# Issuing one layer's raw weight loads from the scalar engine's DMA queue instead of SyncE's

## The chip, the cores and the metric

The kernel runs on one core of a Trainium2 chip. Its time is the device time of one execution in microseconds (us); of several executions the median is given. A core has a matrix engine (PE, with PEld for its weight loads), a vector engine (DVE), a scalar engine (ACT), GpSimd (POOL) and SyncE (SP). SP computes nothing here: it issues DMA transfers. Each engine has one queue of instructions, which it works through in order. An instruction whose semaphore is not there yet holds up all that stands behind it on its engine.

## The reference, cut to what matters

Two layers over a sequence of 512 tokens of width 2048, all in float32. Each layer normalises its input, mixes, multiplies by large weight matrices and adds a gated result. Layer 0 is an attention with forget gates, layer 1 a recurrence (RWKV-7).

```python
for i in range(DEPTH):                                   # DEPTH = 2
    mod = c_act @ w_mod[i] + b_mod[i]
    shift, scale, gate = jnp.split(mod, 3, axis=-1)
    h = rms_norm(x, norm_w[i]) * (1.0 + scale[:, None, :]) + shift[:, None, :]
    ...                                                  # layer 0: fox_branch, layer 1: rwkv7_branch
    x = x + gate[:, None, :] * out

def rwkv7_branch(h, v_first, mu, w_in, ...):             # layer 1
    xx = jnp.pad(h[:, :-1], ((0, 0), (1, 0), (0, 0))) - h
    xr, xk, xv, xg = (h + xx * mu[i] for i in (0, 2, 3, 5))          # and xw, xa
    r = xr @ w_in[0]; k = xk @ w_in[1]; v = xv @ w_in[2]; z = xg @ w_in[3]
    ...                                                  # decay, v, a: small matrices (lora)
    _, y = lax.scan(step, S0, xs)                        # the recurrence over 512 tokens, 32 heads
    ...                                                  # group norm, bonus
    return (y * jax.nn.silu(z)) @ w_out
```

Layer 1 has five 2048 x 2048 matrices: `r`, `k`, `v`, `z` (the gate) and the output.

## The kernel before

**Three matmuls for one.** A float32 product is made of three faster ones. Both operands are split: a high half, which ACT makes by a copy into a shorter format (`act_hi`), and a low half, the rest, which DVE makes by a subtraction. `mm3` then multiplies high by high, low by high and high by low.

**Tiles, units, parts.** Layer 1's matrices are worked through in 74 output tiles of 128 columns: the last 10 tiles of `k` (the first 6 are made by an earlier stage), then 16 each of `r`, `v`, `z` and the output. A tile has 16 units (a unit is 128 rows of the matrix, one `mm3`), and 4 units are one part: 128 x 512 numbers, 256 KB. There are 296 parts. `backbone` goes over the units in a fixed order. At the change from one matrix to the next two tiles are interleaved.

**What a part needs.** `fetch(n)` brings part n. It takes one of three raw buffers (`raw`, `bufs=3`), has SP load the part from memory, and after 4.5 us of the planner's own clock it traces the split: ACT writes `whi`, DVE then writes `wlo` from `raw` and `whi`. Buffers of `whi` and `wlo` are four each. A raw buffer is free again when `wlo` has been written, so the load of part n waits for `wlo` of part n-3. `fetch(n)` is started at the first unit of part n-4. The first four parts are fetched ahead of the first unit, one whole `fetch` after the other: load, `whi`, `wlo`, load, `whi`, `wlo`, and so on.

**The other work.** Between the units the planner (`Flow`) traces the rest of layer 1 as tasks with due times, counted on PE's work: copies of finished tiles, the lora products, the keys with their norms (`keys`: square `sq`, halves `mhi` and `mlo`, a matmul for the mean, then `t`), 32 x 32 inverses, and the recurrence (`stage`, `products`, `recur`, `normed`). Nearly all of it goes through ACT at some point. Results wait in memory between the stages, and SP issues all of those transfers too.

**What sets the order.** `InOrder` wraps an engine. While its `on` is set, each instruction of the engine is put behind the one traced before it. It is set for PE, ACT and DVE in layer 1, and not for SP: the scheduler of the framework orders SP's transfers by its own estimate of when each can start, so a load whose buffer is free may be issued long before the place where it was traced. The wrapper takes every call on the engine, `dma_start` as well:

```python
def __getattr__(self, name):
    f = getattr(self.engine, name)
    def issue(*a, **k):
        with ExitStack() as s:
            if self.on and self.last is not None:
                s.enter_context(self.tc.issue_after(self.last.ins))
            self.last = f(*a, **k)
```

All transfers that SP and ACT issue count on the same eight completion semaphores, in turn, in the order of the schedule. The program makes a transfer wait until the one that used its semaphore before, eight transfers earlier, has landed.

Of the kernel before, what the change touches and what calls it, by code (L numbers as in the profile page):

```python
# [21 lines left out]
WK = 4  # L22
# [109 lines left out]
def body(ctx, tc, a, out, dbg=None, stop=0):  # L132
    nc = tc.nc
    pe, act, dve, pool, sp = (InOrder(tc, e) for e in (nc.tensor, nc.scalar, nc.vector,
                                                       nc.gpsimd, nc.sync))
# [23 lines left out]
    def bank(tag, bufs=None):  # L159
        return cur["p"].tile([P, T], F, tag=tag, bufs=cur["t"][tag], name=tag)  # L160
# [71 lines left out]
    def act_hi(hi, src):  # L232
        act.activation(hi, src, AF.Copy)
# [19 lines left out]
    def mm3(o, w, k, x, first, last, m0=0, m1=P):  # L253
        wh, wl = w
        xh, xl = x
        pe.matmul(o, wh[:, k, m0:m1], xh, start=first, stop=False)
        pe.matmul(o, wl[:, k, m0:m1], xh, start=False, stop=False)
        pe.matmul(o, wh[:, k, m0:m1], xl, start=False, stop=last)
# [30 lines left out]
    def silu_c(mp):  # L289
        cb = mp.tile([P, D], F, name="cb", bufs=1)  # L290
        cs = mp.tile([P, KT], F, name="cs", bufs=1)
        i = act.activation(cs, vecs[:, V_C], AF.Silu)
        return cb, cs, i
# [22 lines left out]
    freed, spent = set(), set()  # L316
    PLEAD = 4

    def backbone(fl, tiles, at, ready, ends, pairs=(), lead=6, pre=()):

        units, i = [], 0
        while i < len(tiles):
            us = [[(n, k) for k in range(t[4] if len(t) > 4 else 0, KT)]
                  for n, t in enumerate(tiles[i:i + 1 + (i in pairs)], i)]
            units += us[0][:PLEAD] if len(us) > 1 else us[0]
            for u, v in zip(us[0][PLEAD:], us[1] if len(us) > 1 else ()):
                units += [u, v]  # L330
            if len(us) > 1:
                units += us[1][KT - PLEAD:]
            i += len(us)
        starts = {}
        for i, k in units:
            starts.setdefault((i, k // WK), (i, k))
        parts = list(starts)
        ws, used = {}, set()

        def fetch(n):  # L340
            i, h = parts[n]
            raw = wp.tile([P, WK, P], F, tag="raw", name="raw", bufs=3)
            sp.dma_start(raw, tiles[i][0][:, h * WK:h * WK + WK, :])
            yield 4.5
            while n and parts[n - 1] not in ws or n > 3 and parts[n - 4] not in used:
                yield 0.2
            hi = wp.tile([P, WK, P], R, tag="whi", name="whi")
            lo = wp.tile([P, WK, P], R, tag="wlo", name="wlo")
            act_hi(hi, raw)
            yield 1  # L350
            dve.tensor_tensor(out=lo, in0=raw, in1=hi, op=OP.subtract)
            ws[parts[n]] = hi, lo

        def ending(task, i):
            yield from task
            freed.add(i)

        for n, w in enumerate(pre):
            ws[parts[n]] = w
        for n in range(len(pre), 4):  # L360
            for _ in fetch(n):
                pass
        for n in range(4, len(parts)):
            at.setdefault(starts[parts[n - 4]], []).append(fetch(n))
        last = {id(t[1]): i for i, t in enumerate(tiles)}
        banks, seen = {}, set()
        for i, k in units:
            src, acts, done, j = tiles[i][:4]
            first = i not in seen
            while first and i > 1 and i - 2 not in freed:  # L370
                fl.t += 0.2
                fl.run()
            if first:
                seen.add(i)
                banks[i] = bank("pj")
                at.setdefault((i, max(k, KT - lead)), []).append(ending(done(j, banks[i], i), i))
            for t in at.pop((i, k), ()):
                fl.start(fl.t, t)
            fl.run()
            while (id(acts), k) not in ready or (i, k // WK) not in ws:  # L380
                fl.t += 0.2
                fl.run()
            mm3(banks[i], ws[i, k // WK], k % WK, acts[k], first, k == KT - 1)
            if k % WK == WK - 1:
                used.add((i, k // WK))
            if last[id(acts)] == i:
                spent.add((id(acts), k))
            if k == KT - 1:
                ends.add(i)
# [6 lines left out]
    with ExitStack() as s0:  # L396
# [7 lines left out]
        with tc.tile_pool(name="st0", bufs=2, reuse_waits="tile") as q:  # L404
# [97 lines left out]
            cb, cs, i = silu_c(cbp)  # L502
# [91 lines left out]
            pre = [zw[3 * NZ + j] for j in range(4)]  # L594
# [3 lines left out]
        fl = Flow()  # L598
        freed.clear()
        ends, cut, lock, sdone, odone, gdone, ready = (set() for _ in range(7))  # L600
# [314 lines left out]
        tiles = [(a["wz"][j], A, zfin, j, KT - WK) for j in range(NZ)]  # L915
# [7 lines left out]
        at = {}  # L923
        n = len(tiles)
        at[n - 2, 0] = [gathering()]
        ready |= {(id(A), k) for k in range(KT)}
        tiles += [(a["wo0"][j], G, output, j) for j in range(KT)]
        backbone(fl, tiles, at, ready, ends, {n - 2, n}, pre=pre)
        fl.drain()
        gst.close()  # L930
# [121 lines left out]
    fl = Flow()  # L1052
# [13 lines left out]
    ends, ups, vd, qd, rd, yd, zd = (set() for _ in range(7))  # L1066
# [756 lines left out]
    ready = {(id(A), k) for k in range(KT)}  # L1823
    at = {}
    tiles = [(a["wk1"][j], A, kept, j) for j in range(KT - NK, KT)]
# [8 lines left out]
    n0, n1, n2, n3 = NK, NK + KT, NK + 2 * KT, NK + 3 * KT  # L1834
    for n, task in ((n0, mixing(1, Ar, A)), (n1, mixing(0, Av, Ar)), (n2, mixing(2, Az, Av)),
                    (n3, gathering())):
        at[n - 2, 0] = [task]
    backbone(fl, tiles, at, ready, ends, {n - i for n in (n0, n1, n2, n3) for i in (0, 2)}, 14)
    fl.drain()


def build(nc, arrays, dbg=(), stop=0):
    a = {k: nc.dram_tensor("in_" + k, v.shape, mybir.dt.from_np(v.dtype),
                           kind="ExternalInput").ap() for k, v in arrays.items()}
    out = nc.dram_tensor("out_0_dram", (KT, P, T), F, kind="ExternalOutput").ap()
    d = {k: nc.dram_tensor("dbg_" + k, s, F, kind="ExternalOutput").ap() for k, s in dbg}
    with tile.TileContext(nc) as tc, ExitStack() as ctx:
        body(ctx, tc, a, out, d, stop)
    return out
# [11 lines left out]
```

## Time and profile before

| | |
|---|---|
| median of 3 runs | 2402.3 us (2398.12 to 2408.5) |
| the profiled execution's own time | 2401.73 us |
| its span in the profile | 2399.9 us |
| mean granted PE clock | 0.982 |
| DMA, mean over the span | 200 GB/s, 480.23 MB |
| layer 1's `backbone` on PE | about 1179 to 2396 us |

The profile is one execution. "Busy" is the time in which an engine works on an instruction; issuing a DMA is not busy time. A row of a timeline has the start in us from the span's beginning, the duration, the engine, the operation, what it writes and reads, a count where rows are merged, and in brackets the idle time just before it with what ended it. A row of the waits has the engine and what it was about to write, what it waited for, and the total in us, the number of times and the longest. In the rows of a window "(x)" is the number of instructions, PEclk the share of the full clock that PE was granted, and the DMA share the mean busy share of the core's 16 DMA engines. `SPq` is a DMA that SP issues. All instructions carry the line of a helper (L90), so groups are told apart by the names of tiles.

### The profile page before, as it was taken

What the parts mean: (1) busy time and instruction counts of PE and PEld (TensorE: products, weight loads), DVE (VectorE), ACT (ScalarE), POOL (GpSimd) and SP (SyncE); (2) the same over time, 40 slices, a digit from 0 to 9 for tenths busy, and PEclk for the clock granted to TensorE, in tenths of its full rate; (3) what the DMA queues carried; (4) which work ended last, traced back from release to release, by engine and by line L of the source; (5) the groups of instructions that cost most, each with busy time, mean ns of one, the idle gap of its engine ahead of it and who ended that gap; (6) DMA issues with size and microseconds to landing.
All of it is one profiled execution on the core that took longest, in us unless ns stands there. A gap on an engine that the chain in (4) does not pass through costs nothing. (4 is left out here: it accounts for less than half of the span.)

```text
span 2399.9 us, 39413 instructions
## 1 busy us (share of the span) xinstructions
PE 2302.2 (96%) x13626; PEld 1807.3 (75%) x13626; DVE 1605.2 (67%) x2850; ACT 1256.5 (52%) x2300; POOL 694.4 (29%) x1114
## 2 busy tenths in 40 slices
PE   6999999999999999998999898899999899999999
PEld 4787777877778778886777676677777677777787
DVE  6886778888888635336797567666476776755322
ACT  4435655555565545225646777763345556665221
POOL 0002333442424210110141208771245535450000
PEclk8999999999999999999999999899999999999999
DMA  8864466766666346445756999886867766544543
GB/s 307 328 227 156 128 211 217 222 213 213 205 224 220 114 161 225 142 141 157 223 179 198 308 263 277 256 252 187 233 187 195 219 174 194 167 132 154 161 137 97
DMA packets 388152, 480.23 MB, mean 200 GB/s; under 512 B 146032, under 2 KB 217840, under 8 KB 384112
## 3 DMA queue, kind: packets, MB, share of 16 engines
q1 hardware_dynamic: 386288, 475.08, 63.7%
q0 software_dynamic: 1664, 2.63, 0.3%
q8 instruction: 108, 1.77, 0.3%
q14 instruction: 92, 0.75, 0.1%
HBM read 381.63 MB, written 95.95 MB: 199 GB/s over the span
## 5 line engine op out<-in xcount | busy, mean ns | idle before, releaser
L90 PE MATMUL pj<-hi,whi 128*128 128x512 f32 x2416 | 987.4, 409 | 11.0 <-ACT hi L90 8.2
L90 PE MATMUL pj<-hi,wlo 128*128 128x512 f32 x2416 | 959.4, 397 | 10.1 <-DVE wlo L90 10.0
L90 PE MATMUL pj<-lo,whi 128*128 128x512 f32 x2416 | 959.9, 397 | 0.0
L90 DVE TENSOR_TENSOR wlo<-raw,whi 128x512 fp32r<-128x512 f32 (+2 forms) x628 | 473.4, 761 | 255.1 <-ACT whi L90 252.4
L90 ACT ACTIVATE whi<-raw 128x512 fp32r<-128x512 f32 (+2 forms) x628 | 393.9, 634 | 399.0 <-PE pj L90 215.1
L90 PEld LDWEIGHTS pj<-hi,whi 128*128 128x128 f32 x2416 | 459.5, 190 | 116.8 <-ACT hi L90 9.2
L90 PEld LDWEIGHTS pj<-lo,whi 128*128 128x128 f32 x2416 | 458.3, 190 | 108.4 <-DVE lo L90 0.7
L90 PEld LDWEIGHTS pj<-hi,wlo 128*128 128x128 f32 x2416 | 459.9, 190 | 105.2 <-DVE wlo L90 13.4
L90 DVE CUSTOM_DVE_ANT_0 wm<-wm,cb 128x1024 f32<-128x1024 f32 x128 | 155.8, 1217 | 0.3
L90 POOL TENSOR_SCALAR SV<-SV,dec 64x64 f32<-64x64 f32 x224 | 94.2, 442 | 103.9 <-DVE SV L90 69.7
L90 ACT ACTIVATE pr<-Sm,mx 128x128 f32<-128x128 f32 (+3 forms) x128 | 71.5, 559 | 76.8 <-POOL mx L90 76.3
L90 POOL TENSOR_SCALAR pr<-pr,rc 128x128 f32<-128x128 f32 (+3 forms) x128 | 100.8, 788 | 26.0 <-DVE rc L90 23.6
L90 POOL TENSOR_SCALAR mx<-mx 128x1 f32<-128x1 f32 x128 | 59.9, 468 | 143.2 <-DVE mx L90 98.0
L90 DVE CUSTOM_DVE_ANT_0 Sm<-S,cmask 128x128 f32<-128x128 f32 (+3 forms) x128 | 62.3, 487 | 42.5 <-PE S L90 41.8
L90 POOL TENSOR_TENSOR lt<-lane 128x30 f32<-128x30 f32 (+14 forms) x90 | 64.2, 713 | 86.4 <-DMA lane<-mld 79.6
L90 POOL TENSOR_TENSOR bk<-bk,eI 128x512 f32<-128x512 f32 x32 | 36.6, 1142 | 110.3 <-PE S L90 64.0
L90 POOL TENSOR_TENSOR lane<-lane,lt 128x30 f32<-128x30 f32 (+14 forms) x90 | 64.0, 711 | 7.0
L90 PE MATMUL S<-k,q 128*128 128x128 f32 (+7 forms) x256 | 61.9, 323 | 0.0
L90 POOL TENSOR_TENSOR acc<-acc,sq 128x512 f32<-128x512 f32 x14 | 18.1, 1296 | 149.4 <-ACT sq L90 128.2
L90 ACT ACTIVATE pT<-tr 128x512 f32<-128x512 f32 x64 | 31.0, 485 | 54.4 <-PE tr L90 54.4
L90 DVE SCALAR_TENSOR_TENSOR hp<-pj,gate,hp 128x512 f32<-128x512 f32 x16 | 12.0, 751 | 68.0 <-PE pj L90 68.0
L90 PE MATMUL tr<-ident,pr 128*128 128x128 f32 x320 | 56.0, 273 | 1.5 <-DVE pT L90 1.3
(325 smaller groups left out, 3284.0 us busy)
## 6 DMA issues: line engine op xcount, KB each, us to landing
wm<-in_wmodT SPq DMA_DIRECT2D x132, 512.0 KB, 4.4
raw<-in_wz SPq DMA_DIRECT2D x128, 256.0 KB, 3.7
raw<-in_wo SPq DMA_DIRECT2D x128, 256.0 KB, 3.6
raw<-in_wv SPq DMA_DIRECT2D x124, 256.0 KB, 3.9
wm<-in_wmodT SPq DMA_DIRECT2D x30, 1024.0 KB, 6.4
raw<-in_wk SPq DMA_DIRECT2D x96, 256.0 KB, 3.7
raw<-in_wr SPq DMA_DIRECT2D x64, 256.0 KB, 5.0
raw<-in_wq SPq DMA_DIRECT2D x56, 256.0 KB, 3.5
```

The lines of the kernel that those rows point to most:

```text
L90: self.last = f(*a, **k)
```

## The change

`backbone` gets a parameter for the engine that issues the raw loads. Layer 0 keeps SP. Layer 1's call passes `act`, so its 296 raw loads become instructions of ACT's queue, and as `act.on` is set they keep the place in ACT's order in which `fetch` traces them.

```diff
-    def backbone(fl, tiles, at, ready, ends, pairs=(), lead=6, pre=()):
+    def backbone(fl, tiles, at, ready, ends, pairs=(), lead=6, pre=(), ld=sp):
...
         def fetch(n):
             i, h = parts[n]
             raw = wp.tile([P, WK, P], F, tag="raw", name="raw", bufs=3)
-            sp.dma_start(raw, tiles[i][0][:, h * WK:h * WK + WK, :])
+            ld.dma_start(raw, tiles[i][0][:, h * WK:h * WK + WK, :])
             yield 4.5
...
-    backbone(fl, tiles, at, ready, ends, {n - i for n in (n0, n1, n2, n3) for i in (0, 2)}, 14)
+    backbone(fl, tiles, at, ready, ends, {n - i for n in (n0, n1, n2, n3) for i in (0, 2)}, 14,
+             ld=act)
```

## The prediction

> **What bounds the kernel now.** I read the shares of the engines first, then windows over layer 1, then the waits of PE, of ACT and of SP there.
>
> ```profile
> PE 2302.2 (96%) x13626; PEld 1807.3 (75%) x13626; DVE 1605.2 (67%) x2850; ACT 1256.5 (52%) x2300; POOL 694.4 (29%) x1114
> ```
>
> PE is the bound: an edit changes the time only where it makes or removes idle time of PE, or clock that PE loses. The next rows cover layer 1's busiest stretch, the rest of it, the change to the output matrix, and two short stretches behind a stall of PE.
>
> ```profile
> 1340.00:1617.00 277.00, 251.42 (x1640) 193.87 (x1640) 182.59 (x242) 194.60 (x358) 153.41 (x212) 0.94 0.90 267
> 1650.00:2190.00 540.00, 522.96 (x5063) 410.85 (x5062) 355.32 (x748) 291.71 (x510) 220.74 (x425) 0.99 0.66 184
> 2190.00:2230.00 40.00, 37.01 (x156) 28.52 (x155) 22.98 (x42) 21.93 (x35) 0.00 (x0) 1.00 0.68 215
> 1561.00:1565.00 4.00, 3.82 (x15) 2.69 (x17) 2.58 (x4) 2.65 (x4) 3.61 (x6) 0.55 1.06 341
> 1920.00:1924.00 4.00, 4.00 (x19) 2.91 (x19) 3.19 (x8) 3.72 (x7) 0.60 (x1) 0.63 0.57 149
> ```
>
> From 1340 to 1617 PE is idle 277 - 251.4 = 25.6 us and is granted 0.94 of its clock, which costs another 277 x 0.06 = 16.6 us: 42 us are lost here, and an idle microsecond costs 1 + 16.6/25.6 = 1.65. The two short rows show why: just behind a stall PE gets 0.55 and 0.63. From 1650 to 2190 only 17 of 540 us are idle.
>
> Whom PE waits for (first three rows: 1340 to 1650; fourth: 1650 to 2230), and what ACT waits for ahead of a weight split (two rows of 1340 to 1650, three of 1650 to 2190):
>
> ```profile
> PE S L90 <- ACT mhi L90: 10.5, 5, 3.9
> PE S L90 <- DVE mlo L90: 8.4, 9, 2.0
> PE pj L90 <- DVE wlo L90: 7.1, 3, 2.8
> PE S L90 <- ACT GP L90: 9.7, 5, 5.3
> ...
> ACT whi L90 <- DMA raw<-in_wr: 33.6, 20, 4.8
> ACT whi L90 <- DMA raw<-in_wv: 7.4, 2, 4.0
> ACT whi L90 <- PE pj L90: 56.6, 33, 3.7
> ACT whi L90 <- DMA raw<-in_wv: 23.8, 13, 5.2
> ACT whi L90 <- DMA raw<-in_wz: 0.4, 1, 0.4
> ```
>
> In the busy stretch PE waits for the halves `mhi` and `mlo` of the keys, and ACT makes `mhi` late because it stands in front of a weight split whose load has not landed: 33.6 + 7.4 = 41 us. Later ACT mostly waits for PE, so it is ahead. SP's own waits in layer 1 (1230 on):
>
> ```profile
> SPq L90 <- DVE wlo L90: 144.4, 130, 7.8
> SPq L90 <- DMA raw<-in_wo: 10.5, 12, 1.3
> ```
>
> SP stands 144 us in front of raw loads whose buffer DVE has not freed, with other transfers queued behind them. The second row is the program's turn of eight semaphores: transfers that read no weight wait for a weight to land.
>
> **The change part by part.** It removes no work. 296 loads (74 tiles x 4 parts) leave SP's queue and enter ACT's, each with its issue time, its wait for the buffer (`wlo` of part n-3) and its turn of the eight semaphores. What SP sheds is off PE's path except where a transfer or a split is late today. What ACT takes on holds up every copy, split and exponential behind it.
>
> Issue times (min/median/max in ns, count last) in layer 1, and the time from issue to landing, first over layer 1, then in 1340 to 1617:
>
> ```profile
> L90 SPq DMA_DIRECT2D raw<-in_wr x64: 333/431/1746, 1357.5 to 1610.9; - x64
> L90 SPq DMA_DIRECT2D raw<-in_wv x64: 328/400/1925, 1613.3 to 1898.0; - x64
> L90 SPq DMA_DIRECT2D raw<-in_wz x64: 327/360/869, 1899.0 to 2198.9; - x64
> DMA to landing us min/median/max: 2.9/4.1/7.4
> DMA to landing us min/median/max: 3.2/5.0/7.4
> ```
>
> No row shows a DMA that ACT issues. Its price on ACT lies between nothing (issued by the sequencer while the last copy still runs) and SP's 0.36 to 0.43 us; I take half.
>
> *Term 1, the start.* The first four parts, and the copies `kt` that free PE's banks behind them:
>
> ```profile
> 1084.93 0.33 SPq L90 DMA_DIRECT2D raw<-in_wk  x1
> 1091.65 0.93 SPq L90 DMA_DIRECT2D raw<-in_wk  x2
> ...
> 1170.90 0.71 ACT L90 ACTIVATE mr<-hp,omu 128x512 f32<-128x512 f32 x1
> 1171.52 1.66 ACT L90 ACTIVATE whi<-raw 128x512 fp32r<-128x512 f32 x3
> 1178.25 0.63 ACT L90 ACTIVATE whi<-raw 128x512 fp32r<-128x512 f32 x1 [5.08 <-DMA raw<-in_wk]
> 1178.79 1.06 ACT L90 ACTIVATE kt<-pj 128x512 f32<-128x512 f32 x2
> ...
> 1179.42 0.51 PE L90 MATMUL pj<-hi,whi 128*128 128x512 f32 x1
> ```
>
> Today three of the loads go out before 1093, as SP's order is free, and only the fourth is waited for. Traced on ACT they stand load, split, load, split, all behind `mr`: four round trips in a row. At 3.5 us each, between the least and the median landing, the fourth split starts at 1171.6 + 4 x 3.6 = 1186.0 instead of 1178.25. `kt` and PE's first matmul follow it 1.2 us later as now. PE, which had just run out of work at 1179.4, then stands idle for 7.8 us more, and loses about 2 us to a lowered clock as in the row of 1920. Taken: +10. With 2.9 us a trip and no loss of clock +5, with 5.0 us +16.
>
> *Term 2, 1340 to 1650, 75 loads.* A wait that goes, and what comes for it. The longest case of each:
>
> ```profile
> 1546.83 1.36 SPq L90 DMA_DIRECT2D raw<-in_wr  x1
> 1554.22 0.63 ACT L90 ACTIVATE whi<-raw 128x512 fp32r<-128x512 f32 x1 [4.26 <-DMA raw<-in_wr]
> ...
> 1600.09 0.62 ACT L90 ACTIVATE hi<-hp 128x512 fp32r<-128x512 f32 x1
> 1606.45 0.69 DVE L90 TENSOR_TENSOR wlo<-raw,whi 128x512 fp32r<-128x512 f32 x1
> ...
> 1630.87 0.62 ACT L90 ACTIVATE whi<-raw 128x512 fp32r<-128x512 f32 x1
> 1638.77 0.69 DVE L90 TENSOR_TENSOR wlo<-raw,whi 128x512 fp32r<-128x512 f32 x1
> ```
>
> The load at 1546.83 stood in SP's queue behind six others, landed at 1554.2 and kept ACT idle for 4.26 us; from ACT's queue it could have gone some 2 us earlier. So the 41 us of landing waits shrink. But `fetch` traces the split 4.5 us of planner time behind its load. When ACT is in step that is 4.9 us, hardly more than the 5.0 us of a landing here; when ACT lags it runs the few instructions between them back to back and then waits for its own load. SP ran ahead of that; ACT can't. I take half of the 41 us as gone: -20. New are the buffer waits at which ACT now stands. The load of part 102 comes behind the half at 1600.09 and needs the buffer whose `wlo` ends at 1607.14: 6.4 us. The load of part 110 comes behind the split at 1630.87 and needs the `wlo` that ends at 1639.46: 8.0 us. With one of 4 us between them: +18. Issue: 75 x 0.43 = 32, half of it covered: +16. ACT's net is +14 us. PE passes on (10.5 + 8.4)/41 = 0.46 of ACT's landing waits today, at 1.65 with the clock: I take 0.4 x 1.65 x 14 = +9. If the issue is covered and all landing waits go: (18 - 41) x 0.66 = -15. If neither: (18 + 32) x 0.66 = +33.
>
> *Term 3, 1650 to 2190, about 120 loads.* Issue 120 x 0.38 = 46, half covered: +23 on ACT. The 23.8 us of `in_wv` halve: -12. The `in_wz` splits wait for nothing today; in the plan some loads come to stand just ahead of their own split:
>
> ```profile
> 2014.66 0.63 ACT L90 ACTIVATE whi<-raw 128x512 fp32r<-128x512 f32 x1
> ```
>
> This split (part 188) follows a copy `z` directly, and its load would come between the two and be waited for in full, 4.1 us. About a dozen of the 64 stand so close, at 2 us each: +25. Buffer waits, by the same reading as above, one of 6 us and a few shorter: +13, an estimate. ACT's net is +49 us, but ACT is 54% busy here (291.7 of 540) and ahead of PE, so I let a tenth through: +5, with -4 (SP's other loads come earlier) and +15 as bounds.
>
> *Term 4, 2190 to 2230.* At the change to the output matrix DVE is late:
>
> ```profile
> 2207.09 1.14 ACT L90 ACTIVATE hi<-hp 128x512 fp32r<-128x512 f32 x2
> 2210.81 0.69 DVE L90 TENSOR_TENSOR wlo<-raw,whi 128x512 fp32r<-128x512 f32 x1
> ```
>
> A load traced ahead of these halves needs the buffer of this `wlo`, so they and the tile copy behind them start about 4.3 us later, while PE waits for weights at 2211 already. Taken +3, from 0 to +6.
>
> *Term 5, the output tiles from 2230 on*, is nothing. ACT is mostly idle:
>
> ```profile
> 2248.28 0.63 ACT L90 ACTIVATE whi<-raw 128x512 fp32r<-128x512 f32 x1 [2.16 <-PE pj L90]
> 2253.86 0.63 ACT L90 ACTIVATE whi<-raw 128x512 fp32r<-128x512 f32 x1 [2.16 <-PE pj L90]
> ```
>
> A load that follows the first split has 4.95 us until its own at 2253.86, and landings there are short. If it came 2 us late, PE would still have its weights, which lie ready for about 7 us.
>
> Sum: 10 + 9 + 5 + 3 = +27 on the profiled execution's 2401.7 us (span 2399.9): 2428.7, say 2428. The median of the runs is 2402.3, so the execution stands for it. Ends: +5 - 15 - 4 + 0 = -14 and +16 + 33 + 15 + 6 = +70.
>
> **The rivals.**
>
> *Faster: the loads land in time.* SP is free of 144 us of buffer waits and of the issue of 296 loads, a weight no longer queues behind six other transfers, and the issue hides under ACT's copies. Terms 1, 3 and 4 stay at +18. Term 2 must fall under -30 for a gain of 0.5%. With all 41 us gone, 18 us of buffer waits, and all of it passed on at 1.65, it is -38: 2382 us. The row of 1554.22 speaks for it; against it, that PE gets less than half of ACT's waits, and that the DMA engines are at 0.90 there already. By the Trainium skill, "DMA: Bandwidth & Descriptors", section "Queues, rings and completion order", each DMA engine takes its queue rows in turn, packet by packet, so loads on ACT's own row would be served beside SP's backlog instead of after it; that is this rival, and no row shows two such queues at once. Chance 0.18.
>
> *No change.* The landing waits that go pay for what ACT takes on (term 2 at -5, terms 3 and 4 at +1), and the start alone is left, in part: 2401.7 + 6 = 2408. What speaks for it is that PE's weights lie ready for several us nearly everywhere. The same page, section "Issuing engines are not separate DMA queues", says that issuing from several engines saves only the sequencer's time to start a transfer; by that rule alone the change is worth nothing to PE, which doesn't wait for SP, and the time would stay at 2402. Chance 0.20.
>
> *Much slower: ACT becomes the bound in term 2.* ACT is 194.6 of 277 us busy there. If each of the 68 loads costs 0.43 us, and ACT, once it lags, waits 1 us for its own load each time, that is 97 us more on it. If its idle 82 us take 70 of them, the other 27 at 1.65 are 45 us, and with terms 1, 3 and 4 unchanged it is 2401.7 + 18 + 45 = 2465. The turn of eight semaphores adds to it: a load on ACT waits for SP's transfer eight places before, and SP's for ACT's. Chance 0.12.
>
> That the change doesn't do what it says is excluded by the wrapper, which fixes the place of each load on ACT.
>
> **How the numbers follow.** Forecast 0.50, much slower 0.12, no change 0.20, faster 0.18. Half a per cent (12 us) is about what a measurement of this kernel can tell from no change. Slower 0.62, same 0.20, faster 0.18. The likeliest case alone runs from 2412 to 2450. The range that leaves out two in ten takes the lower end from the bounds (2401.7 - 14 = 2388) and the upper end from the much slower case: 2388 to 2465.
>
> **What would show it.** Term 1: the first matmul of layer 1 at about 1187 instead of 1179.4, with ACT waiting for `in_wk` three or four times ahead of it and a lowered clock behind. Term 2: the busy time of PE in 1340 to 1650, moved by term 1; ACT's waits for `in_wr` under 33.6 us; ACT idle before instructions that follow a load, ended by DVE's `wlo`. Term 3: ACT's waits for `in_wz`, now 0.4. Term 4: idle time of PE at the change of matrix, over 3 us. SP's waits for `wlo` should fall to near nothing. I am wrong if PE starts layer 1 on time, or if its lost time in 1340 to 1650 falls by more than 20 us.

## The result and the profile after

The changed kernel takes 2421.8 us (median of 8 runs, 2413.46 to 2428.37) against 2401.35 us (8 runs, 2398.12 to 2408.5) for the kernel before on the same chip. The ratio is 1.008, with a 95% interval of 1.0062 to 1.0098: slower by 20 us. The profiled execution took 2418.0 us, with a span of 2416.2.

The profile page's row of engine shares and its rows of DMA queues (packets, MB, share of 16 engines) for the changed kernel:

```profile
PE 2302.3 (95%) x13626; PEld 1807.4 (75%) x13626; DVE 1600.5 (66%) x2850; ACT 1258.0 (52%) x2300; POOL 695.6 (29%) x1114
q1 hardware_dynamic: 343664, 397.46, 51.7%
q10 hardware_dynamic: 42624, 77.61, 11.7%
```

PE is busy for the same 2302 us, so nearly all of the 16 us of span are idle time. q10 is new: 77.61 MB, the 296 loads of layer 1. Windows over the same stretches as in the prediction, moved by 10, 24 and 24 us to hold the same work at their start, and below them the clock at the large stall:

```profile
1350.00:1627.00 277.00, 240.35 (x1608) 185.71 (x1607) 167.35 (x219) 189.27 (x345) 144.00 (x207) 0.93 0.87 254
1674.00:2214.00 540.00, 527.87 (x5103) 415.45 (x5102) 362.01 (x761) 298.95 (x522) 226.41 (x426) 1.00 0.67 184
2214.00:2254.00 40.00, 36.54 (x147) 27.97 (x147) 19.65 (x32) 16.76 (x28) 0.00 (x0) 0.96 0.64 204
1485.00:1513.00 28.00, 6.53 (x26) 5.34 (x27) 4.00 (x6) 7.92 (x15) 9.86 (x22) 0.51 0.47 129
```

In the busy stretch PE works 240.4 us instead of 251.4: 11 more us are lost. In the long stretch behind it PE works 527.9 instead of 523.0: that one became better. The waits of PE from 1350 to 1674 (first four rows) and from 1674 to 2254 (fifth), then ACT's ahead of weight splits (two of 1350 to 1674, two of 1674 to 2205), then SP's from 1230 on:

```profile
PE S L90 <- ACT t L90: 23.7, 1, 23.7
PE pj L90 <- DVE wlo L90: 6.6, 3, 4.4
PE S L90 <- ACT mhi L90: 5.9, 7, 2.3
PE S L90 <- DVE mlo L90: 5.9, 10, 1.7
PE S L90 <- ACT GP L90: 5.0, 4, 2.8
...
ACT whi L90 <- DMA raw<-in_wr: 10.8, 11, 1.7
ACT whi L90 <- DMA raw<-in_wv: 2.0, 1, 2.0
ACT whi L90 <- DMA raw<-in_wz: 14.2, 8, 3.3
ACT whi L90 <- DMA raw<-in_wv: 13.8, 8, 3.8
...
SPq L90 <- DVE wlo L90: 9.9, 19, 1.3
SPq L90 <- DMA qld<-lane: 44.6, 3, 30.8
```

Most of the waits of before are smaller: `mhi` and `mlo` cost PE 11.8 us instead of 18.9, `GP` 5.0 instead of 9.7, and SP's 144 us in front of raw buffers are 10. One wait is new, and it alone is larger than the whole loss: PE stands once for 23.7 us at `t`. The timelines of four engines around it, in the order of cause and effect:

```profile
1450.50 0.24 POOL L90 TENSOR_TENSOR lt<-lane 128x30 f32<-128x30 f32 x1 [64.51 <-DMA lane<-mld]
1496.07 0.63 POOL L90 DMA_DIRECT2D qld<-lane  x1 [0.30 <-POOL lane L90]
...
1467.92 0.32 SPq L90 DMA_DIRECT2D mxd<-m  x1
1499.12 0.81 SPq L90 DMA_DIRECT2D qt<-qld  x2
...
1500.60 0.63 SPq L90 DMA_DIRECT2D ip<-ipd  x1
...
1476.12 0.62 ACT L90 ACTIVATE mhi<-sq 128x512 fp32r<-128x512 f32 x1
1504.09 0.34 ACTq L90 DMA_DIRECT2D raw<-in_wr  x1
1504.47 0.72 ACT L90 ACTIVATE m<-hp,omu 128x512 f32<-128x512 f32 x1 [27.73 <-DMA ip<-ipd]
1505.73 0.69 ACT L90 ACTIVATE t<-S,nfloor 128x512 f32<-128x512 f32 x1
...
1506.47 2.07 PE L90 MATMUL S<-at,bk 64*128 64x128 f32 x14 [23.65 <-ACT t L90]
```

POOL inverts the first group of 32 x 32 blocks from 1450.5 on and stores them (`qld`) at 1496. SP stands from 1468 to 1499 at two loads that read this store. Behind them stands an `ip` load. ACT's next instruction after `mhi` is a raw load, whose only wait in the program is its turn: the transfer eight places earlier is that `ip` load, issued at 1500.60 and landed 3.5 us later, at 1504.1. So ACT stands, and with it `m`, `t`, and PE.

The two loads are not part of the change. In the kernel before SP issued all eight of that kind at once, after `qld` had landed, and waited for it 2.7 us in all of layer 1:

```profile
1494.42 0.63 POOL L90 DMA_DIRECT2D qld<-lane  x1 [0.30 <-POOL lane L90]
...
1502.83 4.74 SPq L90 DMA_DIRECT2D qt<-qld  x8
...
SPq L90 <- DMA qld<-lane: 2.7, 2, 1.6
```

PE's, DVE's and ACT's computing instructions have the same order in both kernels. POOL's differ in 19 places of 1076, and it has the order of the changed kernel in the first three experiments too, with the stall and without it. SP's transfers are ordered by the scheduler's own estimate, and with the raw loads out of the queue that estimate put the first two `qt` loads behind seven `at` stores instead of ten.

How far the changed kernel lies behind, at the same matmul of each (start in the kernel before, then the lag): first of layer 1, 1179.42, 10.9 us; 1461.87, 6.1; 1477.49, 32.4; 1567.78, 22.8; 1660.77, 24.1; 1752.60, 19.6; 1949.83, 14.6; 2201.98, 14.6; 2214.21, 17.8; from 2240 to the end 16.4. Of the first 10.9 us, 4.7 are there at the matmul just ahead, before PE needs a load that ACT issued; 2.5 of them arose between 220 and 300 us, where the changed kernel's profile has a stretch of half clock that the other has not. In two kernels below the first matmul of layer 1, with its loads on SP, comes 2.2 us late and 1.9 us early, so the 4.7 us are taken as scatter.

### The profile page after: what moved, and what is told of

Its sections match the earlier page's. It is cut to its first block, busy times and chain, and to the rows that moved or that the text cites. A ratio compares the mean times of both kernels' runs of the same rounds, so it can differ in the third digit from the quotient of the medians.

```text
span 2416.2 us, 39379 instructions
## 1 busy us (share of the span) xinstructions
PE 2302.3 (95%) x13626; PEld 1807.4 (75%) x13626; DVE 1600.5 (66%) x2850; ACT 1258.0 (52%) x2300; POOL 695.6 (29%) x1114
## 3 DMA queue, kind: packets, MB, share of 16 engines
q10 hardware_dynamic: 42624, 77.61, 11.7%
```

## The experiments

All times are medians; the ratio is to the kernel before, run beside it (2402.7 us for the first four, 2401.8 for the other four), with its 95% interval.

**The qt loads put back.** Each `qt` load of SP is ordered behind the latest `bkd` store traced before it:

```diff
+            bks.append(sp.dma_start(bkd[...], ...))
...
-                    sp.dma_start(qt[RS[p][b], :, 32 * b:32 * b + 32], qld[...])
+                    with tc.issue_after(bks[-1].ins):
+                        sp.dma_start(qt[RS[p][b], :, 32 * b:32 * b + 32], qld[...])
```

> The changed kernel, with one thing set back: each of SP's 64 qt<-qld loads is ordered behind the latest bkd<-bk store written before it, which gives the first 16 of them the place in SP's order that they have in the kernel before (behind ten at stores, not behind seven). The order of PE, DVE and ACT stays that of the changed kernel. Theory A (SP stands on the early qt loads for the inverse that POOL needs 45 us for, and a raw load on ACT waits for an ip load queued behind them): the 23.65 us gap of PE at 1506 and its half clock go, less the 8 us that the changed kernel wins back behind it: 2395 to 2408 us, 14 to 27 under the changed kernel. Theory B (ACT is made late by its own 296 issues and by the waits for raw buffers; the gap is where that came out): the time stays, 2415 to 2425 us, with a gap of PE elsewhere in 1450 to 1650.

2392.2 us (0.9962, 0.9949 to 0.9975): 30 us under the changed kernel, and 3 below theory A's range. PE's largest sum of waits, its longest single wait, and SP's wait for `qld`, in this kernel:

```profile
PE S L90 <- DVE mlo L90: 13.4, 14, 2.4
PE pj L90 <- ACT kt L90: 7.1, 1, 7.1
...
SPq L90 <- DMA qld<-lane: 15.2, 3, 8.1
```

The 23.7 us wait for `t` is gone, and no wait of its size has come in its place, which theory B needed; the longest is the 7.1 us of the start. With the `qt` loads in place the change makes the kernel 0.4% faster than before.

**The start put back.** Only the first four raw loads go to SP again:

```diff
-            ld.dma_start(raw, tiles[i][0][:, h * WK:h * WK + WK, :])
+            (ld if n >= 4 else sp).dma_start(raw, tiles[i][0][:, h * WK:h * WK + WK, :])
```

> The changed kernel, with the first four raw loads of layer 1 back on SP and the other 292 on ACT. Theory A: the first pj matmul of layer 1 stands where it stood relative to the stage ahead of it (6.3 us of idle time go, perhaps 2 us of half clock more), the stand of SP at the qt loads stays: 2412 to 2417 us, 5 to 9 under the changed kernel. Rival (the later start is the half clock of earlier stages and the load latency, not the queue): no change, 2420 to 2424 us.

2416.2 us (1.0055, 1.0035 to 1.0075), 5.5 under the changed kernel, as theory A has it; but the intervals of the two overlap, so this run alone does not show a gain in time. What it shows is the place: the first `pj` matmul of layer 1 follows the matmul ahead of it without a gap, and the stand at `t` is still there:

```profile
1177.31 0.39 PE L90 MATMUL S<-lo,whi 128*128 128x512 f32 x1
1177.54 0.40 PE L90 MATMUL pj<-hi,whi 128*128 128x512 f32 x1
...
PE S L90 <- ACT t L90: 24.7, 2, 24.4
```

**Both put back.**

> Both of these together: qt loads ordered behind the latest bkd store, first four raw loads on SP, the other 292 on ACT. Theory A: the two savings add up, 2388 to 2402 us, at or under the kernel before, since what is left of the change (fewer waits for SP's place in 1340 to 1650 and 1650 to 2190) was a gain of about 5 and 9 us in the changed kernel's trace. Theory B: not under 2410 us.

2387.1 us (0.9934, 0.9920 to 0.9948), just below theory A's range: faster than both kernels. The savings add up: the start is worth 5.5 us without and 5.1 with the `qt` repair, the `qt` place 29.6 without and 29.1 with the start. Between the two versions with the `qt` loads in place the start's gain is clear of the scatter: their ratios differ by 0.0028, and the 95% interval of that difference, worked out from the two intervals, is 0.0019 to each side. What is left of the change, 292 loads on ACT, is a gain of 15.6 us.

**The stall without the change.** In the kernel before, all raw loads on SP, two `qt` loads are put as early as in the changed kernel, and left out at their old place:

```diff
+            if j == 3:
+                fl.start(fl.t + INV - 28, early())
...
+    def early():
+        for b in range(2):
+            with tc.issue_after(bks[-1].ins):
+                sp.dma_start(qts[0][32 * b:32 * b + 32, :, 32 * b:32 * b + 32], qld[...])
...
+                    if j == 0 and p == 0:
+                        continue
```

The other 62 `qt` loads are ordered behind the latest `bkd` store, where they stand in the kernel before anyway.

> The kernel before, all raw loads on SP, with the first two of its 64 qt<-qld loads put early: behind seven at stores instead of ten, as the changed kernel has them. Nothing else is moved. Theory A: SP stands at them until POOL's inverse has landed, about from 1462 to 1498, and the raw loads, ip loads and r stores behind them stand with it: 2415 to 2435 us. Rival (a stand of SP is harmless while the raw loads are its own, because only a raw load on ACT carries it to ACT): 2400 to 2406 us.

2425.6 us (1.0095, 1.0078 to 1.0112), 23 over the kernel before. SP, ACT and PE in this kernel:

```profile
1463.91 0.52 SPq L90 DMA_DIRECT2D rTd<-r  x1
1491.92 0.81 SPq L90 DMA_DIRECT2D qt<-qld  x2
...
1496.00 0.63 ACT L90 ACTIVATE whi<-raw 128x512 fp32r<-128x512 f32 x1 [26.23 <-DMA raw<-in_wr]
...
1497.39 1.86 PE L90 MATMUL S<-at,bk 64*128 64x128 f32 x13 [22.03 <-ACT t L90]
```

SP stands at the same two loads until `qld` has landed. Here the raw load itself stands behind them, ACT waits for it, and PE's gap is 22.0 us. So the misplaced loads alone, with no raw load moved, make a loss of 23 us, and the turn of semaphores is only the road by which it reached ACT in the changed kernel; with the raw loads on SP it gets there by the queue. In the changed kernel their place is worth 29 us; where the other 6 us come from stays open.

**Where the remaining gain sits.** The version with both repairs, with ACT issuing the loads of the `k` and `r` tiles only (`ld if 4 <= n and i < 26 else sp`), and its counterpart with those of the `v`, `z` and output tiles only (`i >= 26`):

> The version with both repairs (qt loads behind the latest bkd store, first four loads on SP), with the raw loads on ACT for the k and r tiles alone (100 of 296); those of the v, z and output tiles are SP's again. The question is where that version's 15.6 us under the kernel before come from. Theory A (all of layer 1 gains, as the changed kernel's trace showed it: about 7 us by 1700 and as much again by 2000): 2393 to 2399 us. Rival (the gain is the r stretch alone, where SP is fullest): 2385 to 2390 us, the whole of it.

> The counterpart: the k and r loads (104) on SP, those of the v, z and output tiles (192) on ACT, qt loads behind the latest bkd store (where they stand in the kernel before anyway). Theory A: the other half of the gain, 2391 to 2398 us. Rival (the gain is the r stretch alone): 2400 to 2406 us, the kernel before.

2392.9 us (0.9964, 0.9950 to 0.9977) and 2391.1 us (0.9961, 0.9949 to 0.9973): 9 and 11 us under the kernel before: theory A in both, though the first lies 0.1 us below its range. The two gains make 20 us, the whole was 15.6; the difference is within the intervals. Waits of PE from 1650 to 2250, first two rows the kernel before, last two the counterpart:

```profile
PE S L90 <- ACT GP L90: 9.7, 5, 5.3
PE S L90 <- ACT mhi L90: 3.5, 1, 3.5
...
PE S L90 <- ACT GP L90: 3.8, 3, 2.0
PE S L90 <- ACT mhi L90: 0.9, 1, 0.9
```

The largest of these, in the kernel before and then in the counterpart:

```profile
1911.91 0.89 SPq L90 DMA_DIRECT2D prk<-ipd  x1
1917.31 0.63 ACT L90 ACTIVATE eI<-prk 128x512 f32<-128x512 f32 x1 [4.09 <-DMA prk<-ipd]
...
1896.91 0.61 SPq L90 DMA_DIRECT2D prk<-ipd  x1
1902.91 0.63 ACT L90 ACTIVATE eI<-prk 128x512 f32<-128x512 f32 x1 [0.83 <-DMA prk<-ipd]
```

ACT had finished what stands ahead of `eI` at 1913.22 and at 1902.08. SP issued the `prk` load 1.3 us ahead of that in the first kernel, and 5.2 us in the second, where no raw load stood among the transfers in front of it. This is a transfer other than a weight that became earlier relative to the work that needs it. All ten kernels bear that out: PE's gap at this place is 4.1 to 6.1 us in the four in which SP issues the `z` loads, and 1.7 to 2.8 in the six in which ACT does. The smaller gain, at `mhi`, is a weight's: in the kernel before ACT stood 3.1 us at a split for `in_wv` just ahead of it.

**The price of an issue on ACT.** Both repairs, each raw load on ACT split into two halves:

```diff
-            ld.dma_start(raw, tiles[i][0][:, h * WK:h * WK + WK, :])
+            if n < 4 or ld is sp:
...
+            else:
+                for p in range(0, WK, 2):
+                    ld.dma_start(raw[:, p:p + 2], tiles[i][0][:, h * WK + p:h * WK + p + 2, :])
```

> The version with both repairs, with each of the 292 raw loads on ACT split into two loads of half the size, so that ACT issues 292 more. Theory A (an issue on ACT costs no ACTIVATE time: in the changed kernel's trace the step from one ACTIVATE to the next was the same, within 0.02 us, with an issue between them and without): 2385 to 2392 us, 0 to 5 over the version with whole loads. Rival (an issue takes 0.33 us of ACT, as its own row has it, half of it covered, as the prediction took it): 48 us more ACT time, a tenth to four tenths of it passed on: 2393 to 2408 us.

2398.7 us (0.9989, 0.9974 to 1.0003), 11.5 over the version with whole loads: theory A missed it, and the time lies in the rival's range. Whether it is the rival's mechanism, 0.33 us of ACT for every issue, the trace has to tell. Issues on ACT in the changed kernel (min/median/max in ns), then ACT with halves:

```profile
L90 ACTq DMA_DIRECT2D raw<-in_wr x64: 334/335/559, 1365.4 to 1637.2; - x64
...
1450.00 1.40 ACTq L90 DMA_DIRECT2D raw<-in_wr  x2
1451.45 1.57 ACT L90 ACTIVATE gab<-S 64x256 f32<-64x256 f32 x4 [2.20 <-DMA bkd<-bk]
```

I took the places where two ACTIVATEs follow each other within 0.15 us in the kernel before, and compared the pause there. In the version with whole loads one issue lies in 145 of these places; the pause is longer by 0.000 us in the median and by at most 0.001 in three quarters of them. With halves, two issues lie in a row in 92 of them: 0.006 in the median, over 0.6 in a quarter, 54 us in sum. So a single issue does not by itself take 0.33 us of ACT, as the rival needs, and two in a row often cost something. Some of that is the second issue, some of it turns of the semaphores, as in the row above, where ACT waited for a `bkd` store. The halves also land otherwise (2.2/3.5/7.9 us min/median/max against 2.9/3.9/6.9), and ACT's idle time ahead of `in_wv` splits grew from 18.4 to 30.1 us. How the 11.5 us divide stays open.

**Other transfers off SP.** The kernel before, with the 64 `mld<-gab` stores on ACT's queue and the raw loads on SP:

```diff
-                sp.dma_start(mld[j // 4, l:l + 8].rearrange("c s t -> s c t"), ...)
+                act.dma_start(mld[j // 4, l:l + 8].rearrange("c s t -> s c t"), ...)
```

> The kernel before, all raw loads on SP; instead of them the 64 mld<-gab stores of the r stretch go to ACT's queue, behind the gab copies that ACT has just made; qt loads behind the latest bkd store, so that their place is that of the kernel before. Theory R (the gain of the repaired version in the r stretch is SP's relief: whatever leaves SP's queue there brings the loads and stores behind it forward): 2394 to 2400 us. Rival (the gain is the raw loads' own, which no longer wait for their place in SP's order): 2400 to 2406 us.

2413.4 us (1.0051, 1.0039 to 1.0063): slower, which neither theory expected. ACT in this kernel, then its waits for r weights from 1340 to 1650:

```profile
1410.62 2.76 ACTq L90 DMA_DIRECT2D mld<-gab  x3
1413.48 0.81 ACT L90 ACTIVATE aa<-aa,oka,vecs 128x512 f32<-128x512 f32 x1 [3.86 <-DMA mld<-gab]
...
ACT whi L90 <- DMA raw<-in_wr: 10.8, 8, 3.5
```

The waits for `in_wr` fall from 33.6 to 10.8 us although the raw loads stayed on SP. That may be SP's relief, or only that ACT, itself late, finds its weights landed. ACT is late because the stores come in fours and it stands at them, here for 3.9 us; 8 of the 15 us by which this kernel's profile is late arise from 1350 to 1440. The run does not tell the two theories apart, as its loss on ACT covers both.

## Why the prediction was right, and where it was not

The forecast was 2428, in the range 2388 to 2465; measured are 2421.8. The sign and the size are right, but the size, and the sign with it, by luck. Of the five terms the first is right by its mechanism, the last rightly nothing; the loss in the second has another cause than the one given. Terms 2 to 4 were taken at +17, and with the start and the `qt` loads put back what is left of the change is a gain of 15.6 us. Some 29 us that stood in no term made up for that. With the `qt` loads alone in place the same change comes out at 2392.2, faster than before.

*Term 1, the start, +10.* Right in kind. The four loads and splits stand one behind the other (first and last split of the four, and the first matmul, in the changed kernel):

```profile
1179.12 0.63 ACT L90 ACTIVATE whi<-raw 128x512 fp32r<-128x512 f32 x1 [2.84 <-DMA raw<-in_wk]
...
1189.18 0.63 ACT L90 ACTIVATE whi<-raw 128x512 fp32r<-128x512 f32 x1 [2.70 <-DMA raw<-in_wk]
1190.34 0.80 PE L90 MATMUL pj<-hi,whi 128*128 128x512 f32 x1 [6.30 <-ACT kt L90]
```

The three trips between these splits take 10.06 us, 3.35 each, the idle time 6.3 us instead of 7.8. By the time it is worth 5.1 to 5.5 us, the lower end of 5 to 16: the 2 us of clock behind it were given back by 1350, where the lag is that of the first matmul again.

*Term 2, 1340 to 1650, +9.* The lag went from about 11 to 24 us, +13, but not for the reasons given. The issues, taken at +16 on ACT, cost nothing at the median place (the 145 places above). The buffer waits, taken at +18, sum to 3 us in this stretch, none over 2 (from the end of the ACTIVATE before to the issue, where a `wlo` ends just ahead of it): the three places taken did not come back at their size. The landing waits, taken as halved from 41 us, fell to 12.8; that is not the stall's doing, as in the version with both repairs those for `in_wr` are 8.3. Without the misplaced loads the term is a gain: in the two versions with the `qt` loads put back the lag changes by -8.3 and -9.0 us over this stretch, within the bounds, on the side of the lower end of -15. What made it positive, about 26 us at one place, was in no term. The step that failed stands at the head of the part on the change, "What SP sheds is off PE's path except where a transfer or a split is late today": what SP sheds also changes the order of what stays with it. The sum put that at nothing; it measured 29 us. The front matter says that the scheduler orders SP by its own estimate, and I used that for the raw loads only.

*Term 3, 1650 to 2190, +5.* The lag fell by 9.5 us, beyond the lower end of -4. The issues, 23 us in the sum, fall under the same finding. ACT's waits for `in_wz`, expected at 25 us, are 14.2, and those for `in_wv` fell from 23.8 to 13.8 where 11.9 was taken. The buffer waits on ACT were 22 us where 13 was taken. Little of this can have reached PE, as its lag fell. Mis-sized was what SP's relief is worth, bounded at 4 us: PE's waits for `GP` and for the `mhi` of the recurrence alone fell from 13.2 to 6.6 us.

*Term 4, +3,* measured +1.7 (14.6 to 16.4, after 3.1 in between). *Term 5,* nothing: the lag is 16.38 us from 2240 to the end.

*The rivals.* The faster one had the sign of the rest right, with the issue hidden and the loads in time: with the start and the `qt` loads put back, 15.6 us are gained. Its sizes were off: it had all of the gain in term 2, at -38, where 8 to 9 us were gained, and term 3 at +5, where another 9.5 were gained. It lost to two side effects. The much slower one named, in half a sentence, the road of the stall (the turn of eight semaphores), but no single place for it, and its main term, an issue at 0.43 us of ACT each, was not found. On the two rules of the Trainium skill, "DMA: Bandwidth & Descriptors": ACT's loads do appear as a queue row of their own (q10), as "Queues, rings and completion order" has it, but a load landed hardly sooner for that. From issue to landing layer 1's raw loads took 2.9/4.0/7.0 us (min/median/max) on ACT's row, and 2.9/4.1/7.4 on SP's; in the busy stretch the medians are 4.7 and 5.0. So far the trace agrees with "Issuing engines are not separate DMA queues". That only the sequencer's issue time is saved falls short here, where 15.6 us were gained: SP's 144 us of waits at raw buffers left its queue as well. How much of the gain is owed to either was not tested.

The time of the change so divides into +5.5 (start), +29 (`qt` loads) and -15.6 (the rest). These make +19, against the +20.4 of the result; they must, as each is a difference between neighbouring versions, and the 1.4 is the difference between two medians of the kernel before.

## What to carry to other kernels

Moving transfers off a queue that a scheduler orders moves the others too. Compare the order of what stays behind, above all of loads whose producer takes far longer than its neighbours, and pin those. A transfer on a computing engine is cheap if it can go the moment it is reached; it is dear where several follow in a row or where it waits, by a shared completion semaphore, for a queue that may stand.

## What the hardware showed

A DMA issue on ACT takes 0.334 us by its own row. When it stands alone between two ACTIVATEs that follow each other closely, it adds nothing to the pause between them in the median, and at most 0.001 us in three quarters of 145 places. The Trainium skill, "Perfetto Trace Analysis", section "DVE / Act Engine Instruction (TENSOR_ADD, Activation, etc)", has the sequencer push an instruction into a wait queue, from which it moves to an execution FIFO ahead of the engine, and be ready for the next one after the push; the 145 places agree with that.

The granted clock fell to a half 2.5 us into the stall and stayed there until 6 us behind its end (0.51 in the window 1485 to 1513). Of those 28 us only the last six, with PE at work again, cost time, about 3 us. This long stall so cost little more than its own length, while the 1.65 per idle microsecond of the prediction came from some twenty stalls of at most 3.9 us.
